# A hybrid decoder layer on one core: the decays' mask moves to GpSimd, the memory's transposes are issued later, and the last stage multiplies before its norm

## The chip, the cores and the metric

One Trainium2 chip, of which one core is used. The metric is the device time of one execution in microseconds (us). It is the median of three runs, and one further execution was profiled.

## The reference, cut to what matters

One decoder layer on x (1 x 1024 x 1024, float32): a root-mean-square norm, a projection to eleven parts, three branches (gated DeltaNet, differential attention, cross-attention to a memory of 256 rows), a gated sum, an output projection and a norm with the residual added.

```python
h = rms_norm(x, pre_w)
(gdn_qkv, gdn_a, gdn_b, gdn_z, dq, dk, dv, dz, mq, mz, gate_logits) = [h @ w_in[:, lo:hi] for lo, hi in bounds]
qkv = jax.nn.silu(causal_depthwise_conv(gdn_qkv, conv_w))
...
# inside the gated DeltaNet, by chunks
G = jnp.cumsum(gc, axis=-1)
gamma = jnp.exp(jnp.where(incl, G[..., :, None] - G[..., None, :], -jnp.inf))
a_low = jnp.where(strict, bc[..., :, None] * kk * gamma, 0.0)
...
attn_intra = jnp.einsum("bnhcd,bnhed->bnhce", qc, kc) * gamma
...
m = rms_norm(mem, mem_norm_w)
mk, mv = jnp.split(m @ w_mem_kv, 2, axis=-1)
...
out = y @ w_out
return x + rms_norm(out, post_w)
```

`gamma` is the masked decay that the first part of the change is about, `m` the memory's norm of the second, and the last line the third.

## The kernel before, in words

The sequence of 1024 positions lies along the free axis of most tiles, features along the 128 partitions. The program goes through stages on one core: the input projections with the DeltaNet of 8 heads (to about 550 us), the memory's norm, keys and values (about 550 to 590 us), the attention projections, the attention and the branches' merge, and the output projection with its norm (from about 1840 us).

**Projections.** `gemm` (L209) multiplies a weight block of 128 columns with the normed input into one of two PSUM tiles `acc` (128 x 1024). A weight block is loaded in two pieces (`wr`), and `wsplit` (L161) splits each piece in two for precision: ACT casts the high part `wh` (L167), DVE subtracts for the low part `wl` (L169). The products of `wh` are L219 and L220, those of `wl` L224; one weight column block of 128 rows takes four 512-column matmuls of `wh` and then two of `wl`. So PE can start a gemm with `wh` alone and needs `wl` after four matmuls.

**Heads.** `conv_head` (L430) evacuates such an `acc`: ACT writes the first tap (L435), DVE adds three more taps reading the same PSUM tile (L437, three instructions one after the other), ACT applies SiLU (L439). `key`, `qry` and `val` do that for the key, query and value of each head. Beside a key or query runs a thread (`key_side`, `qry_side`): `decay` (L461) loads the cumulative decays of a head into a 128 x 1024 tile by DMA (L463), waits two steps, adds the mask `mneg` on DVE (L465), waits a step, and ACT takes eight exponentials (L468, one per chunk of 128). `chunk_products` (L470) lets PE multiply chunks into a PSUM tile `sd` (L474), DVE multiplies by the decays (L476) and sums diagonals (L480). There are 8 heads with 2 decays each, so 16 masks. `squares` transposes on PE (L449) and squares on ACT (L457). POOL (GpSimd) computes powers (`rpow`, L158) and products with a whole tile: L504 (a key's decays times `fj`), L629 (a query times a decay), L691 and L692 (power and product at the end of a pair of heads' scan). `inverses` (L512) solves on DVE with many small instructions (L528, L529).

**What sets the order.** The threads are generators. `count` (L183) advances all of them one step whenever six big matmuls have been issued, and `pause(n)` (L201) lets n steps pass. Then a scheduler orders each engine's instructions, so that they don't stand in the order of the code: an engine runs its own list in order, and a later instruction waits behind an earlier one that isn't ready. A change of engine or pause therefore moves neighbours too.

**Memory.** `mem_norm` (L744) loads two tiles of 128 rows (`raw`), ACT squares, POOL raises to a power (L158), DVE scales (L760); after `pause(3)` (L762) PE transposes the tiles in 16 instructions (L767), ACT and DVE split the result (L771, L772). `mem_keys` and `mem_values` use it (L784, L795 to L797). The threads of `combine_tokens` (L818 to L828 on POOL and DVE, then L742 on DVE) work beside it.

**Last stage.** For each of 8 tiles of 128 rows PE fills two halves `po` (128 x 512, PSUM); ACT squares each half with a sum (L1438), DVE adds the sums (L1440), POOL raises to -1/2 (L1441), and for each half DVE multiplies with the norm and the weight (L1443); the residual is added by POOL for half 0 and DVE for half 1 (L1444), and a DMA writes the half (L1445).

Of the kernel before, what the change touches and what calls it, by code (L numbers as in the profile page):

```python
# [9 lines left out]
F32 = mybir.dt.float32  # L10
F32R = mybir.dt.float32r
AF = mybir.ActivationFunctionType
ALU = mybir.AluOpType
# [3 lines left out]
P = 128  # L17
# [7 lines left out]
NEG = -1.0e30  # L25
# [20 lines left out]
def bm(ap, m):  # L46

    return ap.unsqueeze(1).to_broadcast([ap.shape[0], m, ap.shape[1]])
# [3 lines left out]
def hybrid_layer_kernel(  # L52
# [10 lines left out]
    def pool(name, bufs=1, space=None):  # L63
        kw = {} if space is None else {"space": space}
        return tc.tile_pool(name=name, bufs=bufs, **kw)
# [4 lines left out]
    op = ctx.enter_context(pool("op"))  # L70
# [40 lines left out]
    def sd():  # L111
        return sidp.tile([P, 4, P], F32, name=nm("sd"), tag="sd", bufs=4)

    def small(shape, tag, bufs=2, dt=F32):
        return sm.tile(list(shape), dt, name=nm(tag), tag=tag, bufs=bufs)
# [4 lines left out]
    V, A, G, T = nc.vector, nc.scalar, nc.gpsimd, nc.tensor  # L120
# [80 lines left out]
    def pause(n):  # L201
        for _ in range(n):
            yield
# [72 lines left out]
    with gx:  # L276
        gp = gx.enter_context(pool("gp"))
# [7 lines left out]
        tri = gp.tile([P, P], F32, name="tri")  # L285
        G.memset(tri, 1.0)
        G.affine_select(tri, tri, pattern=[[1, P]], compare_op=ALU.is_ge, fill=0.0, base=0, channel_multiplier=-1)
        mneg = gp.tile([P, P], F32, name="mneg")
        G.memset(mneg, 0.0)
        G.affine_select(mneg, mneg, pattern=[[1, P]], compare_op=ALU.is_ge, fill=NEG, base=0, channel_multiplier=-1)  # L290
        ones = gp.tile([P, P], F32, name="ones")
        G.memset(ones, 1.0)

# [167 lines left out]
        def decay(h, gm):  # L461

            nc.sync.dma_start(gm, gscr[0, 8 * h:8 * h + 8, :].rearrange("c i -> (c i)").partition_broadcast(P))  # L463
            yield from pause(2)
            V.tensor_tensor(gm, gm, bm(mneg, 8), op=ALU.add)  # L465
            yield from pause(1)
            for c in range(8):
                A.activation(gm[:, c], gm[:, c], AF.Exp, bias=negG[:, h, c:c + 1])  # L468
# [253 lines left out]
    def xtile(shape=(P, S), dt=F32):  # L722
        return xp.tile(list(shape), dt, name=nm("x"), tag="x", bufs=9)

    def rtile(shape=(P, S), dt=F32):
        return xp.tile(list(shape), dt, name=nm("raw"), tag="raw", bufs=3)
# [8 lines left out]
    SUB, ADD, MUL = ALU.subtract, ALU.add, ALU.mult  # L735
# [8 lines left out]
    def mem_norm():  # L744

        mts = []
        for t in range(2):
            mt = rtile((P, D))
            nc.sync.dma_start(mt, mem[t * P:(t + 1) * P, :])
            mts.append(mt)  # L750
        for _ in range(2):
            mh.append(xtile((P, 4, MEM), F32R))
            ml.append(xtile((P, 4, MEM), F32R))
        sq = rtile()
        for mt in mts:
            ss = small([P, 1], "ss", 4)
            A.activation(sq, mt, AF.Square, accum_out=ss)
            rs = small([P, 1], "rs", 4)
            rpow(rs, ss, 1.0 / D, EPS, mhalf)
            V.tensor_scalar(mt, mt, rs, None, op0=MUL)  # L760
            yield
        yield from pause(3)  # L762
        for k2 in range(4):
            pt = sd()
            for kk in range(2):
                for t in range(2):
                    T.transpose(pt[:, 2 * kk + t], mts[t][:, (2 * k2 + kk) * P:(2 * k2 + kk + 1) * P], ident)  # L767
            for kk in range(2):
                k = 2 * k2 + kk
                src = pt[:, 2 * kk:2 * kk + 2].rearrange("p a b -> p (a b)")  # L770
                A.activation(mh[k // 4][:, k % 4], src, AF.Copy, scale=memw[:, k:k + 1])  # L771
                V.scalar_tensor_tensor(ml[k // 4][:, k % 4], src, memw[:, k:k + 1],  # L772
                                       mh[k // 4][:, k % 4].bitcast(F32), op0=MUL, op1=SUB)
            yield
        ready.add("mem")
# [294 lines left out]
    base = xtile()  # L1070
# [341 lines left out]
    pw = xtile()  # L1412
# [16 lines left out]
    for t in range(NT):  # L1429

        ts_ = slice(t * P, (t + 1) * P)
        po = pos[t] if t < 2 else columns()
        xr, res = xtile(), xtile()
        nc.sync.dma_start(xr, x[ts_, :])
        ss = small([P, 2], "oss", 4)
        for f, sl in enumerate(half):
            products(po, t, range(4 if t < 2 else 0, KT), f)
            A.activation(res[:, sl], po[f], AF.Square, scale=1.0 / 32, accum_out=ss[:, f:f + 1])  # L1438
        rs = small([P, 1], "rs", 4)
        V.tensor_scalar(rs, ss[:, 0:1], ss[:, 1:2], EPS, op0=ADD, op1=ADD)  # L1440
        G.tensor_tensor(rs, rs, mhalf[:, 0:1], op=ALU.pow)  # L1441
        for f, sl in enumerate(half):
            V.scalar_tensor_tensor(res[:, sl], po[f], rs, pw[:, sl], op0=MUL, op1=MUL)  # L1443
            (V if f else G).tensor_tensor(res[:, sl], res[:, sl], xr[:, sl], op=ADD)  # L1444
            nc.sync.dma_start(out[ts_, sl], res[:, sl])  # L1445


# [22 lines left out]
```

## Time and profile before

| | |
|---|---|
| median of three runs | 1926.06 us (1922.33 to 1928.35) |
| the profiled execution | 1924.15 us |
| its span in the trace | 1922.4 us |
| mean granted TensorE clock | 0.992 of full speed |
| busy PE (matmul) | 1868.7 us, 97% of the span |
| busy DVE | 1218.5 us, 63% |
| busy ACT | 894.5 us, 47% |
| busy POOL | 164.0 us, 9% |

The span is from the first to the last instruction of the profiled execution; its own time is 1.75 us longer. PE is TensorE's matmul, DVE VectorE, ACT ScalarE, POOL GpSimd, SP the engine whose queue issues the DMAs. Busy time overlaps between engines. A wait is an engine's idle time, put down to the work that ended it.

### The profile page before, as it was taken

The numbers are of one execution on the slowest core, as the hardware profiler recorded it, in microseconds if no ns is written. First come the engines' busy times: TensorE is split into PE (matmuls) and PEld (weight loads), VectorE is DVE, ScalarE is ACT, GpSimd is POOL, SyncE is SP. The second block draws the span as 40 slices with busy tenths as digits, with TensorE's granted clock in tenths as the row PEclk, the third lists the DMA queues.
The fourth block names the chain that finished last, engine by engine and source line by source line (L and its number), as shares of the span: only waits on it lengthen the run. The fifth ranks groups of instructions, "written<-read, shape, count | busy, mean of one in ns | idle before, by whom it ended". The sixth has DMA issues, their size and how long they took to land.

```text
span 1922.4 us, 28495 instructions
## 1 busy us (share of the span) xinstructions
PE 1868.7 (97%) x10231; PEld 1561.9 (81%) x10231; DVE 1218.5 (63%) x2499; ACT 894.5 (47%) x1997; POOL 164.0 (9%) x131
## 2 busy tenths in 40 slices
PE   7999999999978999999999999999999999999998
PEld 5787888788866888888888888888888878888886
DVE  5688667855366676777777777766666662435432
ACT  5552664545444465555555565555444551212211
POOL 1130131302140100000000000000000000000011
PEclk9999999999989999999999999999999999999999
DMA  4232231322136675656657355443665586755422
GB/s 129 87 97 68 69 96 42 98 63 75 51 120 200 190 210 171 173 162 184 185 143 212 114 176 170 148 154 104 214 207 188 170 270 206 231 195 171 156 91 88
DMA packets 294018, 282.45 MB, mean 147 GB/s; under 512 B 41474, under 2 KB 226164, under 8 KB 293876
## 3 DMA queue, kind: packets, MB, share of 16 engines
q1 hardware_dynamic: 293876, 280.63, 47.4%
q8 instruction: 80, 1.31, 0.3%
q14 instruction: 62, 0.51, 0.1%
HBM read 189.27 MB, written 91.29 MB: 146 GB/s over the span
## 4 chain that ended last, share of the span: by engine, by line
PE 57%; issue 30%; DVE 8%; ACT 2%; DMA 2%; POOL 1%; SPq 0%; POOLq 0%; DVEq 0%; ACTq 0%
PE bank L878 27%; PE acc L224 4%; PE acc L220 4%; PE acc L219 4%; PE sd L1191 3%; PE sd L1143 2%; PE sd L1142 2%; PE sd L1176 2%; DVE o L437 1%; DVE wl L169 1%; PE sd L474 1%; DMA wr<-in_w_mem_kv_dram 1%; PE sd L661 1%; PE sd L673 1%; PE sd L668 1%
## 5 line engine op out<-in xcount | busy, mean ns | idle before, releaser
L878 PE MATMUL bank<-h,hi 128*128 128x512 f32 x864 | 283.7, 398 | 0.0
L167 ACT CAST wh<-wr 128x512 fp32r<-128x512 f32 x144 | 89.3, 620 | 281.6 <-PE acc L220 251.6
L219 PE MATMUL acc<-h,wh 128*128 128x512 f32 x468 | 194.1, 415 | 2.2 <-DVE rp L157 1.8
L220 PE MATMUL acc<-h,wh 128*128 128x512 f32 x468 | 186.7, 399 | 0.0
L878 PE MATMUL bank<-q,hi 128*128 128x512 f32 x576 | 186.4, 397 | 0.0
L878 PE MATMUL bank<-o,hi 128*128 128x512 f32 x576 | 185.2, 396 | 0.8 <-DVE u L965 0.4
L878 PEld LDWEIGHTS bank<-h,hi 128*128 128x128 f32 x864 | 159.5, 188 | 28.2
L878 PE MATMUL bank<-h,lo 128*128 128x512 f32 x432 | 171.4, 397 | 0.0
L224 PE MATMUL acc<-h,wl 128*128 128x512 f32 x468 | 159.4, 399 | 9.2 <-DVE wl L169 9.2
L169 DVE TENSOR_TENSOR wl<-wr,wh 128x512 fp32r<-128x512 f32 x144 | 102.7, 714 | 101.3 <-ACT wh L167 97.8
L864 ACT CAST hi<-wr 128x512 fp32r<-128x512 f32 x144 | 89.0, 618 | 133.2 <-PE bank L878 112.9
L868 DVE TENSOR_TENSOR lo<-wr,hi 128x512 fp32r<-128x512 f32 x144 | 98.9, 687 | 52.8 <-PE bank L878 39.8
L878 PEld LDWEIGHTS bank<-o,hi 128*128 128x128 f32 x576 | 106.4, 188 | 22.1 <-ACT u L883 1.2
L878 PEld LDWEIGHTS bank<-q,hi 128*128 128x128 f32 x576 | 107.0, 188 | 19.9
L878 PE MATMUL bank<-q,lo 128*128 128x512 f32 x288 | 114.5, 398 | 0.0
L878 PE MATMUL bank<-o,lo 128*128 128x512 f32 x288 | 114.2, 396 | 0.0
L224 PEld LDWEIGHTS acc<-h,wl 128*128 128x128 f32 x468 | 88.4, 191 | 29.1 <-DVE wl L169 11.3
L1158 ACT ACTIVATE x<-x,ng 128x256 f32<-128x256 f32 (+7 forms) x128 | 98.8, 774 | 24.7 <-DVE ng L1154 24.7
L864 ACT CAST hi<-raw 128x512 fp32r<-128x512 f32 x108 | 66.9, 619 | 84.9 <-PE bank L878 79.6
L219 PEld LDWEIGHTS acc<-h,wh 128*128 128x128 f32 x468 | 89.3, 191 | 17.4 <-issue 3.0
L220 PEld LDWEIGHTS acc<-h,wh 128*128 128x128 f32 x468 | 89.3, 191 | 14.5
L878 PEld LDWEIGHTS bank<-h,lo 128*128 128x128 f32 x432 | 81.4, 188 | 14.2
(361 smaller groups left out, 4125.3 us busy)
## 6 DMA issues: line engine op xcount, KB each, us to landing
raw<-in_w_in_dram SPq DMA_DIRECT2D x144, 256.0 KB, 3.8
wr<-in_w_in_dram SPq DMA_DIRECT2D x64, 256.0 KB, 2.8
qd<-u SPq DMA_DIRECT2D x128, 128.0 KB, 2.4
wl<-qd SPq DMA_DIRECT2D x64, 256.0 KB, 3.5
gts<-u SPq DMA_DIRECT2D x48, 256.0 KB, 3.2
u<-oscr SPq DMA_DIRECT2D x48, 256.0 KB, 4.6
raw<-gts SPq DMA_DIRECT2D x24, 512.0 KB, 4.4
o<-gscr SPq DMA_DIRECT2D x16, 512.0 KB, 4.9
```

What stands on the lines that cost most here:

```text
L167: A.copy(hi, raw)
L169: V.tensor_tensor(lo, raw, hi.bitcast(F32), op=ALU.subtract)
L219: T.matmul(ps[:, sl], lhsT=hi[:, kk], rhs=hh(k, f), start=(k == 0), stop=False)
L220: T.matmul(ps[:, sl], lhsT=hi[:, kk], rhs=hl(k, f), start=False, stop=False)
L224: T.matmul(ps[:, sl], lhsT=lo[:, kk], rhs=hh(k, f), start=False, stop=(k == 7))
L864: A.copy(self.hi[p], self.src[p])
L868: V.tensor_tensor(self.lo[p], self.src[p], self.hi[p].bitcast(F32), op=SUB)
L878: T.matmul(ps, lhsT=t[l][:, kk], rhs=comb[p][kk][r], start=(first and kk + n == 0), stop=(kk == 3 and n == 2), skip_group_check=True)
L1142: T.matmul(ps[m], lhsT=q4[:, m], rhs=ks[m][:, u:e], start=True, stop=False)
L1143: T.matmul(ps[m], lhsT=q4[:, 2 + m], rhs=ks[m][:, u:e], start=False, stop=True)
L1158: A.activation(s[i][m][:, :w], s[i][m][:, :w], AF.Exp, bias=ng[:, m:m + 1], scale=scl, accum_out=l)
L1191: T.matmul(po[:, 0], lhsT=pT[:, c], rhs=vt[:, c], start=(c == 0), stop=(c == i))
```

## The change

Three edits. (1) The mask of the decays: `affine_select` on POOL, which fills the masked places with the large negative constant, takes the place of the addition of `mneg` on DVE; the tile `mneg` and its two setup instructions go. (2) `mem_norm` waits nine steps instead of three ahead of its transposes. (3) In the last stage DVE multiplies each half with the weight as soon as the half is there, ACT then squares the half in place in PSUM, and after the norm one DVE instruction per half multiplies by it and adds the residual; POOL's and DVE's additions go.

```diff
--- before.py
+++ after.py
@@ -285,9 +285,6 @@
         tri = gp.tile([P, P], F32, name="tri")
         G.memset(tri, 1.0)
         G.affine_select(tri, tri, pattern=[[1, P]], compare_op=ALU.is_ge, fill=0.0, base=0, channel_multiplier=-1)
-        mneg = gp.tile([P, P], F32, name="mneg")
-        G.memset(mneg, 0.0)
-        G.affine_select(mneg, mneg, pattern=[[1, P]], compare_op=ALU.is_ge, fill=NEG, base=0, channel_multiplier=-1)
         ones = gp.tile([P, P], F32, name="ones")
         G.memset(ones, 1.0)
 
@@ -462,7 +459,8 @@
 
             nc.sync.dma_start(gm, gscr[0, 8 * h:8 * h + 8, :].rearrange("c i -> (c i)").partition_broadcast(P))
             yield from pause(2)
-            V.tensor_tensor(gm, gm, bm(mneg, 8), op=ALU.add)
+            G.affine_select(gm, gm, pattern=[[0, 8], [1, P]], compare_op=ALU.is_ge, fill=NEG, base=0,
+                            channel_multiplier=-1)
             yield from pause(1)
             for c in range(8):
                 A.activation(gm[:, c], gm[:, c], AF.Exp, bias=negG[:, h, c:c + 1])
@@ -759,7 +757,7 @@
             rpow(rs, ss, 1.0 / D, EPS, mhalf)
             V.tensor_scalar(mt, mt, rs, None, op0=MUL)
             yield
-        yield from pause(3)
+        yield from pause(9)
         for k2 in range(4):
             pt = sd()
             for kk in range(2):
@@ -1435,13 +1433,13 @@
         ss = small([P, 2], "oss", 4)
         for f, sl in enumerate(half):
             products(po, t, range(4 if t < 2 else 0, KT), f)
-            A.activation(res[:, sl], po[f], AF.Square, scale=1.0 / 32, accum_out=ss[:, f:f + 1])
+            V.tensor_tensor(res[:, sl], po[f], pw[:, sl], op=MUL)
+            A.activation(po[f], po[f], AF.Square, scale=1.0 / 32, accum_out=ss[:, f:f + 1])
         rs = small([P, 1], "rs", 4)
         V.tensor_scalar(rs, ss[:, 0:1], ss[:, 1:2], EPS, op0=ADD, op1=ADD)
         G.tensor_tensor(rs, rs, mhalf[:, 0:1], op=ALU.pow)
         for f, sl in enumerate(half):
-            V.scalar_tensor_tensor(res[:, sl], po[f], rs, pw[:, sl], op0=MUL, op1=MUL)
-            (V if f else G).tensor_tensor(res[:, sl], res[:, sl], xr[:, sl], op=ADD)
+            V.scalar_tensor_tensor(res[:, sl], res[:, sl], rs, xr[:, sl], op0=MUL, op1=ADD)
             nc.sync.dma_start(out[ts_, sl], res[:, sl])
```

Lines of the changed kernel are two to three lower than those of the kernel before (L435 is L432, L437 is L434, L439 is L436, L457 is L454, L468 is L466, L480 is L478, L691 is L689, L767 is L765); the select is L462. A tile's number in the listings counts allocations.

The order on ACT between the query and the value of head 0, about 99 to 116 us of the trace before. In these rows `o` is first the query's tile (L435, L439) and then two decay tiles (the query's own and a key's), `e` a tile of squares, `v` the value's tile and `wh` the high part of a weight piece. Before:

```order
L435 ACTIVATE o_957<-acc_853,cols 128x1024
L167 CAST wh_1114<-wr_1112 128x512
L439 ACTIVATE o_957<-o_957 128x1024
L468 ACT_TABLE_LOAD
L468 ACTIVATE o_980<-o_980,negG 128x128 x8
L457 ACTIVATE e_1017<-sd_1012 128x512
L457 ACTIVATE e_1038<-sd_1033 128x512
L468 ACTIVATE o_994<-o_994,negG 128x128 x8
L167 CAST wh_1162<-wr_1160 128x512
L435 ACTIVATE v_1105<-acc_963,cols 128x1024
L167 CAST wh_1219<-wr_1217 128x512
```

With the change:

```order
L432 ACTIVATE o_958<-acc_852,cols 128x1024
L466 ACT_TABLE_LOAD
L466 ACTIVATE o_981<-o_981,negG 128x128
L436 ACT_TABLE_LOAD
L436 ACTIVATE o_958<-o_958 128x1024
L466 ACT_TABLE_LOAD
L466 ACTIVATE o_981<-o_981,negG 128x128 x7
L454 ACTIVATE e_1020<-sd_1015 128x512
L454 ACTIVATE e_1043<-sd_1038 128x512
L466 ACTIVATE o_995<-o_995,negG 128x128 x8
L432 ACTIVATE v_1110<-acc_964,cols 128x1024
L167 CAST wh_1119<-wr_1117 128x512
```

The cast of the gemm that comes next on PE (`wh_1114`, now `wh_1119`) stood behind the query's first tap and ahead of the decays; now it stands behind both decays' exponentials and behind the value's first tap. Two more table loads stand there.

The order on DVE at the same place with the change, from the value's taps on:

```order
L434 SCALAR_TENSOR_TENSOR v_1110<-acc_964,cols,v_1110 128x1023
L478 ISA sd_1081,ssk_1060<-sd_1081,ident 128x128
L478 ISA ssk_1060 128x1
L434 SCALAR_TENSOR_TENSOR v_1110<-acc_964,cols,v_1110 128x1022
L499 TENSOR_SCALAR fj<-ssk_1060 128x8
L157 TENSOR_SCALAR rp_1101<-ssk_1060 128x8
L434 SCALAR_TENSOR_TENSOR v_1110<-acc_964,cols,v_1110 128x1021
L500 RECIPROCAL fj<-fj 128x8
L169 TENSOR_TENSOR wl_1121<-wr_1117,wh_1119 128x512
```

The subtraction for that same gemm (`wl_1121`, whose high part is `wh_1119`) stands behind the three taps of the value. Before the change it stood ahead of them, right behind the two mask additions L465.

The order on POOL at the end of the first scan, about 262 to 272 us of the trace before, with the change:

```order
L690 TENSOR_TENSOR v_1110<-v_1110,sso_1871 128x1024
L689 TENSOR_TENSOR sso_1872<-sso_1872,mhalf 128x8
L690 TENSOR_TENSOR v_1338<-v_1338,sso_1872 128x1024
L462 AFFINE_SELECT o_2525<-o_2525 128x1024
L462 AFFINE_SELECT o_2648<-o_2648 128x1024
```

The select of a later key's decays (`o_2525`) is queued behind the powers and products of the scan's end; before the change that mask was an addition on DVE.

The order on PE at the memory's transposes. Before:

```order
L767 MATMUL sd_5317<-ident,raw_5250 128x128
L767 MATMUL sd_5332<-ident,raw_5250 128x128
L219 MATMUL acc_5237<-h_137,wh_5293 128x512
L220 MATMUL acc_5237<-h_138,wh_5293 128x512
L219 MATMUL acc_5237<-h_137,wh_5293 128x512
L220 MATMUL acc_5237<-h_138,wh_5293 128x512
L767 MATMUL sd_5317<-ident,raw_5252 128x128
L767 MATMUL sd_5317<-ident,raw_5250 128x128
```

With the change:

```order
L220 MATMUL acc_5363<-u_130,wh_5366 128x512
L224 MATMUL acc_5363<-h_128,wl_5368 128x512
L224 MATMUL acc_5363<-u_129,wl_5368 128x512
L765 MATMUL sd_5402<-ident,raw_5277 128x128
L765 MATMUL sd_5402<-ident,raw_5279 128x128
L765 MATMUL sd_5402<-ident,raw_5277 128x128
L765 MATMUL sd_5402<-ident,raw_5279 128x128
L219 MATMUL acc_5363<-h_131,wh_5416 128x512
```

Ahead of the first transpose now stand 30 more 512-column matmuls, the last block of the gemm in hand (`acc_5237`, now `acc_5264`) and the first half of the next (`acc_5363`); and the transposes of the two memory tiles now alternate from the first on.

## Rows read from the trace of the kernel before

**Rows 1.** PE's waits, whole span: who waited, for what, us in total, times, longest.
```profile
PE acc L224 <- DVE wl L169: 9.2, 4, 4.5
...
PE sd L767 <- issue: 9.0, 1, 9.0
...
PE acc L796 <- DVE wl L169: 4.5, 4, 2.9
...
PE acc L219 <- DVE rp L157: 1.8, 1, 1.8
```

**Rows 2.** DVE and PE by time, 69 to 78 us: start, length, instruction, [idle before].
```profile
69.83 1.28 DVE L437 SCALAR_TENSOR_TENSOR y<-acc,cols,y 128x1023 f32<-128x1023 f32 x1
...
74.70 0.79 PE L224 MATMUL acc<-h,wl 128*128 128x512 f32 x1 [3.49 <-DVE wl L169]
...
77.00 0.63 PE L220 MATMUL acc<-u,wh 128*128 128x512 f32 x1
```

**Rows 3.** ACT and POOL by time, 101 to 113 us.
```profile
104.02 0.62 ACT L167 CAST wh<-wr 128x512 fp32r<-128x512 f32 x1 [3.80 <-PE acc L220]
...
105.63 1.28 ACT L468 ACT_TABLE_LOAD   x1
...
106.92 2.46 ACT L468 ACTIVATE o<-o,negG 128x128 f32<-128x128 f32 x8
...
109.28 1.05 ACT L457 ACTIVATE e<-sd 128x512 f32<-128x512 f32 x2
...
110.24 2.44 ACT L468 ACTIVATE o<-o,negG 128x128 f32<-128x128 f32 x8
...
101.77 1.64 POOL L158 TENSOR_TENSOR nk<-rp,phalf 128x8 f32<-128x8 f32 x1 [19.20 <-DVE rp L157]
```

**Rows 4.** DVE by time, 111 to 120 us.
```profile
111.54 0.69 DVE L476 TENSOR_TENSOR o<-sd,o 128x512 f32<-128x512 f32 x1 [0.16 <-ACT o L468]
...
115.23 1.28 DVE L437 SCALAR_TENSOR_TENSOR v<-acc,cols,v 128x1023 f32<-128x1023 f32 x1
...
119.16 0.19 DVE L502 RECIPROCAL fj<-fj 128x8 f32<-128x8 f32 x1
```

**Rows 5.** PE by time, 114 to 116 us.
```profile
114.32 0.39 PE L224 MATMUL acc<-h,wl 128*128 128x512 f32 x1
...
114.78 1.05 PE L474 MATMUL sd<-o,y 128*128 128x128 f32 x8
```

**Rows 6.** Lines L465 and L1075: ns of one (least, median, most), first and last start.
```profile
L465 DVE TENSOR_TENSOR o<-o,mneg x16: 1204/1224/2918, 62.6 to 442.3; 128x1024 f32<-128x1024 f32 x16
...
L1075 POOL TENSOR_SCALAR_AFFINE_SELECT x<-x x1: 1149/1149/1149, 634.8 to 634.8; 128x1024 f32<-128x1024 f32 x1
```

**Rows 7.** POOL and DVE by time, 142 to 147 us.
```profile
142.32 1.29 POOL L629 TENSOR_TENSOR o<-o,e 128x512 f32<-128x512 f32 x1 [1.88 <-DMA e<-gscr]
...
142.68 1.18 DVE L529 TENSOR_TENSOR q<-q,y 128x220 f32<-128x220 f32 x1
...
146.48 0.38 DVE L529 TENSOR_TENSOR q<-q,y 128x231 f32<-128x231 f32 x1
```

**Rows 8.** POOL and ACT by time, 266 to 271 us.
```profile
268.72 1.90 POOL L692 TENSOR_TENSOR v<-v,sso 128x1024 f32<-128x1024 f32 x1
...
267.18 2.45 ACT L468 ACTIVATE o<-o,negG 128x128 f32<-128x128 f32 x8 [3.12 <-DVE o L465]
```

**Rows 9.** DVE by time, 556 to 560 us.
```profile
556.61 0.75 DVE L760 TENSOR_SCALAR raw<-raw,rs 128x1024 f32<-128x1024 f32 x1 [1.67 <-POOL rs L158]
...
558.48 0.75 DVE L760 TENSOR_SCALAR raw<-raw,rs 128x1024 f32<-128x1024 f32 x1 [0.45 <-POOL rs L158]
```

**Rows 10.** Busy us by window: length, PE, PEld, DVE, ACT, POOL; granted clock, DMA share, GB/s.
```profile
550.00:600.00 50.00, 36.51 (x142) 27.24 (x142) 43.56 (x58) 22.99 (x43) 18.79 (x13) 0.86 0.46 141
```

**Rows 11.** All engines by time at the kernel's end.
```profile
1915.01 0.60 ACT L1438 ACTIVATE x<-sd 128x512 f32<-128x512 f32 x1 [4.63 <-PE sd L1419]
...
1918.05 1.20 DVE L1444 TENSOR_TENSOR x<-x,x 128x512 f32<-128x512 f32 x1
```

## The prediction

> **What bounds the kernel.** I read the profile table first: PE is busy 97% of the span, so work taken from DVE, ACT or POOL pays only where PE waits for it. The waits of PE say where that is [rows 1]. About 25 us stand in four groups: gemms that wait for the low part of their weights (`wl`, 9.2 and 4.5 us), one wait of 9.0 us ahead of the memory's transposes, and one of 1.8 us for an `acc` tile. The masks are named nowhere in it. The reader should see that ACT and DVE reach PE by their order: both run their lists in order, and a cast for the next gemm that stands behind the evacuation of the last one comes late. The trace has one clear case. At 69.83 DVE begins the three taps of a key (L437); the subtraction for the gemm already begun stands behind them, and PE idles 3.49 us until 74.70 [rows 2]. The order of before has that pattern once in this stage, with 2.2 us of PE work between the two gemms' neighbouring rows. The order of the change has it three times, the old one and two new.
>
> **Part 1, the mask.** It takes 16 additions from DVE, 1.224 us each by the median, 19.6 us in all, and gives POOL 16 selects [rows 6]. The trace has one select of that shape, 1.149 us, on another tile; I take that. Setup loses two small instructions that nothing waits for: nothing. As PE names no wait for a mask, I count none of the 19.6 us as a direct gain. What counts is the order that follows.
>
> *First place, about 115 us.* Before, the cast `wh` of the next gemm ran at 104.02, ahead of the decays [rows 3]. It now comes after both groups of exponentials and the value's first tap. POOL's power ends at 103.4, so the query's select ends near 104.6; then ACT does one exponential (0.3), a table load (1.28), SiLU (1.0, what lies between the cast and the load before) and another load, and the other seven (2.15) end at 110.6 where the eight ended at 109.4. With the squares (1.05) the key's exponentials start near 111.6, not 110.24: 1.4 us later. DVE's product L476 waits for them; it began at 111.54, so the value's taps start at 116.6 instead of 115.23, and after the 3.93 us that the three took, the reciprocal behind them (0.2) and 0.7 for the subtraction (as long as L476, of the same shape) the new `wl` is there at 121.4 [rows 4]. PE needed it at 114.32; with a group of short products now ahead (0.8 of the 1.05) it comes there at about 115.1 [rows 5]. So 6.3 us of new idle time. The wait costs more than its length: after the 3.49 us a matmul at 77.00 still took 0.63 us, where one takes 0.39 at 114.32 [rows 2, 5], as if at the lower of the clock's two levels, 1.2 in place of 2.4 GHz. Two such matmuls start 0.46 apart at the full clock [rows 5]; some 6 at half lose 6 x 0.2 = 1.2 us. Here I put 1.5. **+7.8 us.**
>
> *Second place, about 25 us later.* The same pattern with the query of head 1. From the query's first tap ACT and DVE need 1.1 (tap, about as SiLU), 4.0 (three taps), 1.3 (solve steps between them), 1.28, 1.0, 1.28, 2.15, 1.05, 1.1 and 0.6 to the next `wh`: 14.9 us. PE has 48 matmuls at 0.23 and about 24 to 32 short ones at 0.1, 13.4 us, and meets another us of waiting for `wl`. An estimate from [rows 3 to 5]: **+2.5 us**, between 0 and 5.
>
> *Third place, about 272 us.* The exponentials of a key started at 267.18, behind a mask on DVE. Its select now stands on POOL behind the products of the scan's end, the last of which ends at 270.62; with 1.15 it is out at 271.8, 4.6 us later [rows 8]. ACT evacuates the last gemm's `acc` right behind those exponentials, and PE's wait of 1.8 us for that tile [rows 1] grows by as much. **+4.6 us.** There are places like it near 350 us and later; in them I see slack and put nothing, leaving them to the upper end.
>
> Sum of part 1: 7.8 + 2.5 + 4.6 = **+14.9 us**. From below: had ACT and DVE slack in all of it, -2. From above, with the late places and the full 18.4 us of selects felt by DVE, +24.
>
> *A rule against it.* While POOL's L629 ran from 142.32 to 143.61, a DVE subtraction of 128x220 with two SBUF inputs took 1.18 us from 142.68, to just behind POOL's end; one of 128x231 with POOL idle took 0.38 [rows 7]. The Trainium skill (SBUF — State Buffer, "SBUF: two separate sides") says that DVE with two SBUF inputs and a GpSimd instruction that reads SBUF share a port pair that one of them holds for its whole instruction, so that the other blocks fully. By that rule, the trace agrees: 0.8 us were lost. In the sum by the row alone a select costs DVE at most its 1.15 us; 16 of them give back 18.4 of the 19.6 us.
>
> **Part 2, the transposes.** PE stood 8.97 us and resumed at 557.57. The transposes wait for the scaled memory tiles, and DVE scales them when POOL's power is out: the first starts at 556.61, the second at 558.48, 0.75 us each [rows 9]. PE does not enter into that, so these moments stay. The 30 matmuls now ahead take 30 x 0.23 = 6.9 us; the transposes alternate, so PE waits for the second tile too, to 559.2, and idles some 3.5 us in place of 9. Gain 5.5, and about 1.5 from the clock, granted at 0.86 in this window [rows 10]. But DVE is busy 43.56 of the 50 us here [rows 10], and the memory's products wait for `wl` again behind it (4.5 us [rows 1]). They come 6 us sooner while DVE's list is no shorter. I take back 3. **-4 us**, between 0 and -9.
>
> **Part 3, the last stage.** Only the last of 8 tiles lies on the path. There a DVE product of about 0.7 now stands between PE's end and the square at 1915.01, and the addition of 1.20 at 1918.05 goes, with the wait behind POOL's own [rows 11]. **-0.7 us**, between -1.5 and 0; in the other seven PE's next tile covers it, and if that cover went each would cost the 0.7.
>
> **Sum.** 14.9 - 4 - 0.7 = +10.2 us on the profiled execution's 1924.15: **1934 us**. That execution lies 1.9 us below the median of the runs shown, inside their spread.
>
> **Rivals.**
>
> *The casts are in time.* If the orders leave more slack than I read (a `wh` may run while PE is still on the gemm before), part 1 is worth -2 to +1 and the rest stays: 1924.15 - 4 to -7 - 0.7 = about 1918 us with half of the memory's gain given back. For it: DVE loses 19.6 us in a stage where it is the engine PE waits for. Against: the pattern at 74.70 [rows 2]. It decides at the first place: if `wl` is there at 115 us, this is the case. This is the rival on the other side.
>
> *One new wait, one lost.* The first place alone is real (+8), the third is hidden, the memory gives 7 and the end 0.7: 1924 to 1929 us, no change. For it: the third place lies where PE has other work of the scan.
>
> *The selects hold DVE.* Each of the 16 delays a DVE cast or tap by up to 1.15 us, as in [rows 7]; if a third of them lie ahead of a late cast, that adds 6 us to my sum: 1940 us. Against: in many places POOL starts when the DMA lands, with DVE on PSUM inputs. The skill's rule on the shared port pair, named above, is this rival's.
>
> *The later transposes do nothing.* If DVE's list bounds the memory stage altogether, part 2 is 0: 1938 us, within the forecast's range.
>
> **Chances.** My forecast 0.35, the selects 0.10, no gain from the memory 0.08: slower, 0.53. One wait for one, no change: 0.22. Casts in time, faster: 0.25. A measurement of this kernel can tell about 0.3%, 5.8 us, from no change. The range takes in the rival on the fast side and part 1's upper bound with some of the memory's gain: 1916 to 1945. The slower cases alone would give 1931 to 1945.
>
> **What would show it.** Right: a PE wait for `wl` of 4 us or more near 115 to 122 us, with one for `wh` ahead of it; a wait for `acc` near 275 that grew to about 6; the wait ahead of the transposes at 2 to 4 us in place of 9, with more waiting in the memory's products behind it. Wrong: no PE wait above 2 us between 100 and 150, or the exponentials of the first scan's end still starting near 267 us. If the waits of PE in the first 550 us add to no more than before, part 1 was mis-read and the first rival has it.

## The result and the profile after

The changed kernel took 1937.87 us as the median of five runs (1935.13 to 1942.02), the kernel before 1927.85 beside it (1922.33 to 1928.35). The ratio is **1.0061 [1.0046, 1.0075]**: slower by 0.6%, about 12 us between the means of the runs (10.0 between the medians). The forecast was 1934 in 1916 to 1945. The profiled execution shown below took 1937.87 us, with a span of 1936.2 us and a granted clock of 0.988.

The first part of the profile's page of the changed kernel: busy us of each engine, share of the span, instructions.

```profile
PE 1874.2 (97%) x10231; PEld 1567.5 (81%) x10231; DVE 1200.9 (62%) x2491; ACT 902.1 (47%) x2003; POOL 166.1 (9%) x137
```

DVE has 17.6 us less to do than before, POOL 2.1 more, and the kernel is longer. What grew is PE's waiting. The waits of PE in the changed kernel (who waited for what, us in total, times, longest):

```profile
PE acc L224 <- DVE wl L169: 12.5, 5, 4.4
...
PE acc L793 <- ACT wh L167: 6.0, 2, 4.3
PE acc L794 <- DVE wl L169: 4.5, 4, 3.4
...
PE acc L219 <- ACT wh L167: 3.8, 3, 1.8
PE acc L219 <- DVE rp L157: 3.3, 1, 3.3
...
PE sd L765 <- DVE raw L758: 1.5, 1, 1.5
```

Against [rows 1]: the waits for a gemm's `wl` rose from 9.2 to 12.5 (3.2 of these lie in the memory stage, further down), waits for `wh` are new (3.8), and the 9.0 ahead of the transposes is 1.5. But the memory's keys now wait 6.0 for `wh` at L793, where they waited 2.1 before (L795 there). In the first 545 us all of PE's waits make 31.6 us, and made 23.3 before. So the trace has a loss in that stretch, and a gain in the memory stage that came back as another wait.

**The first place.** ACT by time in the changed kernel, 106 to 119 us:

```profile
106.87 0.40 ACT L466 ACTIVATE o<-o,negG 128x128 f32<-128x128 f32 x1 [2.97 <-POOL o L462]
107.29 1.28 ACT L436 ACT_TABLE_LOAD   x1
...
113.98 2.44 ACT L466 ACTIVATE o<-o,negG 128x128 f32<-128x128 f32 x8
116.32 1.10 ACT L432 ACTIVATE v<-acc,cols 128x1024 f32<-128x1024 f32 x1
117.32 1.13 ACT L167 CAST wh<-wr 128x512 fp32r<-128x512 f32 x2
```

DVE by time, 118 to 124 us:

```profile
121.55 1.27 DVE L434 SCALAR_TENSOR_TENSOR v<-acc,cols,v 128x1021 f32<-128x1021 f32 x1
...
122.85 0.64 DVE L169 TENSOR_TENSOR wl<-wr,wh 128x512 fp32r<-128x512 f32 x1
```

PE by time, 117 to 125 us:

```profile
117.98 0.50 PE L219 MATMUL acc<-h,wh 128*128 128x512 f32 x1 [1.24 <-ACT wh L167]
...
118.78 0.39 PE L220 MATMUL acc<-u,wh 128*128 128x512 f32 x1
123.54 0.79 PE L224 MATMUL acc<-h,wl 128*128 128x512 f32 x1 [4.37 <-DVE wl L169]
124.13 0.63 PE L224 MATMUL acc<-u,wl 128*128 128x512 f32 x1
```

The reader should follow one weight piece. Its cast `wh` ran at 104.02 before [rows 3]. Now it runs at 117.32, behind the exponentials of two decays and the value's first tap on ACT, and PE waits 1.24 us for it. Its subtraction stands behind the value's three taps on DVE and runs at 122.85, and PE waits 4.37 more. Afterwards a matmul takes 0.63 us where it took 0.39, the mark of the clock's lower level: the granted clock is 0.52 from 123.54 to 129.54.

Where a gemm's first tap on ACT (L435, now L432) follows the gemm at once, it tells how late the program is. Three such taps, one ahead of the place, one behind it and one behind the next place. Before, and then in the changed kernel:

```profile
99.11 1.11 ACT L435 ACTIVATE o<-acc,cols 128x1024 f32<-128x1024 f32 x1
...
127.10 1.11 ACT L435 ACTIVATE o<-acc,cols 128x1024 f32<-128x1024 f32 x1
...
165.24 1.11 ACT L435 ACTIVATE y<-acc,cols 128x1024 f32<-128x1024 f32 x1
```

```profile
101.48 1.11 ACT L432 ACTIVATE o<-acc,cols 128x1024 f32<-128x1024 f32 x1
...
137.57 1.11 ACT L432 ACTIVATE o<-acc,cols 128x1024 f32<-128x1024 f32 x1
...
177.85 1.11 ACT L432 ACTIVATE y<-acc,cols 128x1024 f32<-128x1024 f32 x1
```

The program is 2.4 us late ahead of the place and 10.5 us behind it. (The value's own taps, at 116.32 and 150.48, can't be used: there ACT comes late itself, behind the exponentials and squares.) This place costs **8.1 us**: 5.6 of waiting, and some 2.5 of matmuls that start 0.43 us apart instead of 0.23.

**The second place.** PE by time, 151 to 155 us: the same pattern with smaller waits, 2.1 us together. At 177.85 the program is 12.6 us late, where it was 10.5: **2.1 us**.

```profile
152.14 0.50 PE L219 MATMUL acc<-h,wh 128*128 128x512 f32 x1 [0.77 <-ACT wh L167]
...
154.68 0.50 PE L224 MATMUL acc<-h,wl 128*128 128x512 f32 x1 [1.34 <-DVE wl L169]
```

**The third place.** POOL and ACT by time, 275 to 281 us:

```profile
275.37 1.90 POOL L690 TENSOR_TENSOR v<-v,sso 128x1024 f32<-128x1024 f32 x1
277.23 3.19 POOL L462 TENSOR_SCALAR_AFFINE_SELECT o<-o 128x1024 f32<-128x1024 f32 x3
...
278.35 2.45 ACT L466 ACTIVATE o<-o,negG 128x128 f32<-128x128 f32 x8 [6.67 <-POOL o L462]
```

The selects do stand behind the scan's last product on POOL. But the program is 11.7 us late here, so on the clock of before the exponentials begin at 278.35 - 11.7 = 266.65, against 267.18 [rows 8]. PE waits more at the spot (3.3 us for `rp`, which was 1.8 [rows 1], and 1.75 for a `wh` at 282, which is new), yet the gemms' first taps are 11.72 us late at 237.23 and 11.68 at 295.85. Between these two taps PE has 306 matmuls to do, where it had 339, so part of the scan's work was done earlier and makes room for the waits. From one tap to the other this place costs nothing.

**The memory stage.** PE by time in the changed kernel, 564 to 593 us:

```profile
564.65 0.50 PE L224 MATMUL acc<-h,wl 128*128 128x512 f32 x1 [1.82 <-DVE wl L169]
...
571.34 0.55 PE L765 MATMUL sd<-ident,raw 128*128 128x128 f32 x3 [1.52 <-DVE raw L758]
...
574.22 1.22 PE L224 MATMUL acc<-h,wl 128*128 128x512 f32 x2 [1.41 <-DVE wl L169]
...
588.80 0.80 PE L793 MATMUL acc<-wh,x 128*128 128x512 f32 x1 [4.34 <-ACT wh L167]
592.97 0.80 PE L794 MATMUL acc<-wl,x 128*128 128x512 f32 x1 [3.38 <-DVE wl L169]
```

The wait of 9.0 us became four (1.82, 1.52, 1.41 and 4.34: 9.1 us), and the last one, 3.38, was 2.9 before [rows 1]. The stage's rows in the view of PE's waits, added (from 545 us to 655, the later end since the program is late), make 17.1 us before and 17.1 after. The window of [rows 10], in the changed kernel (length, PE, PEld, DVE, ACT, POOL; granted clock, DMA share, GB/s):

```profile
550.00:600.00 50.00, 37.51 (x150) 28.94 (x149) 43.24 (x53) 22.98 (x42) 25.49 (x18) 0.83 0.41 121
```

The clock is no better (0.83, 0.86 before). At the first product of the next stage (L878, now L876) the program is 13.0 us late, so the memory stage gave nothing and cost about 1.

**The kernel's end.** All engines by time: DVE's product, then ACT's square in PSUM.

```profile
1929.12 0.69 DVE L1436 TENSOR_TENSOR x<-sd,x 128x512 f32<-128x512 f32 x1 [4.75 <-PE sd L1417]
1929.91 0.58 ACT L1437 ACTIVATE sd<-sd 128x512 f32<-128x512 f32 x1 [4.75 <-DVE x L1436]
```

From here to the span's end are 1936.2 - 1929.12 = 7.1 us. Before, from the square at 1915.01 [rows 11] to 1922.4, it was 7.4: 0.3 us gained.

### The profile page after: what moved, and what is told of

Its sections match the earlier page's. It is cut to its first block, busy times and chain, and to the rows that moved or that the text cites. A ratio compares the mean times of both kernels' runs of the same rounds, so it can differ in the third digit from the quotient of the medians.

```text
span 1936.2 us, 28510 instructions
## 1 busy us (share of the span) xinstructions
PE 1874.2 (97%) x10231; PEld 1567.5 (81%) x10231; DVE 1200.9 (62%) x2491; ACT 902.1 (47%) x2003; POOL 166.1 (9%) x137
## 4 chain that ended last, share of the span: by engine, by line
PE 82%; DVE 8%; issue 3%; ACT 3%; DMA 2%; POOL 1%; SPq 0%; DVEq 0%; POOLq 0%; ACTq 0%
PE bank L876 31%; PE acc L219 9%; PE acc L224 9%; PE acc L220 8%; PE sd L1417 4%; PE sd L1189 3%; PE sd L1141 2%; PE sd L1140 2%; PE sd L1174 2%; PE sd L1291 1%; PE sd L1258 1%; PE sd L472 1%; DVE wl L169 1%; PE sd L659 1%; PE sd L671 1%
## 5 line engine op out<-in xcount | busy, mean ns | idle before, releaser
L876 PE MATMUL bank<-h,hi 128*128 128x512 f32 x864 | 283.7, 398 | 0.0
L876 PE MATMUL bank<-q,hi 128*128 128x512 f32 x576 | 186.5, 397 | 0.0
L876 PE MATMUL bank<-o,hi 128*128 128x512 f32 x576 | 185.2, 396 | 1.0 <-DVE u L963 0.7
L876 PEld LDWEIGHTS bank<-h,hi 128*128 128x128 f32 x864 | 159.5, 188 | 28.2
L224 PE MATMUL acc<-h,wl 128*128 128x512 f32 x468 | 160.1, 401 | 12.5 <-DVE wl L169 12.5
L876 PE MATMUL bank<-h,lo 128*128 128x512 f32 x432 | 171.5, 397 | 0.0
L876 PEld LDWEIGHTS bank<-o,hi 128*128 128x128 f32 x576 | 106.4, 188 | 22.3 <-ACT u L881 1.2
L876 PEld LDWEIGHTS bank<-q,hi 128*128 128x128 f32 x576 | 107.0, 188 | 19.9
L876 PE MATMUL bank<-q,lo 128*128 128x512 f32 x288 | 114.5, 398 | 0.0
L876 PE MATMUL bank<-o,lo 128*128 128x512 f32 x288 | 114.1, 396 | 0.0
L876 PEld LDWEIGHTS bank<-h,lo 128*128 128x128 f32 x432 | 81.4, 188 | 14.1
```

The lines of the kernel that those rows point to most:

```text
L224: T.matmul(ps[:, sl], lhsT=lo[:, kk], rhs=hh(k, f), start=False, stop=(k == 7))
L876: T.matmul(ps, lhsT=t[l][:, kk], rhs=comb[p][kk][r], start=(first and kk + n == 0), stop=(kk == 3 and n == 2), skip_group_check=True)
```

## The experiments

The theory: the loss is all part 1's, and comes from the order it brings (casts behind evacuations), not from the select's length; part 2's wait only moved. The rivals: the selects hold DVE; the parts act on each other; the memory stage waits because DVE's list is too long.

### The three parts alone

Part 1 alone is the first hunk of the change and the lost tile (e1), and e2 has all but this:

```diff
-            V.tensor_tensor(gm, gm, bm(mneg, 8), op=ALU.add)
+            G.affine_select(gm, gm, pattern=[[0, 8], [1, P]], compare_op=ALU.is_ge, fill=NEG, base=0,
+                            channel_multiplier=-1)
```

Part 3 alone (e3) is the last stage's hunk, and part 2 alone (e7) the pause:

```diff
-            A.activation(res[:, sl], po[f], AF.Square, scale=1.0 / 32, accum_out=ss[:, f:f + 1])
+            V.tensor_tensor(res[:, sl], po[f], pw[:, sl], op=MUL)
+            A.activation(po[f], po[f], AF.Square, scale=1.0 / 32, accum_out=ss[:, f:f + 1])
...
-            V.scalar_tensor_tensor(res[:, sl], po[f], rs, pw[:, sl], op0=MUL, op1=MUL)
-            (V if f else G).tensor_tensor(res[:, sl], res[:, sl], xr[:, sl], op=ADD)
+            V.scalar_tensor_tensor(res[:, sl], res[:, sl], rs, xr[:, sl], op0=MUL, op1=ADD)
```

```diff
-        yield from pause(3)
+        yield from pause(9)
```

Part 1 alone:

> The kernel before with part 1 alone: the masks are selects on POOL; pause and last stage as before. The order of the first 545 us is that of the changed kernel. Order theory: the whole loss is here, the cumulated delay of the changed kernel at 500 us, some 11 us (10.8 after taking off the 0.9 us by which its first gemms already began later): 1936 to 1940 us, with PE waits of 1.2 + 4.4 us near 118 and 124 us. Rival (the loss is shared by parts 2 or 3): under 1932 us.

Parts 2 and 3 without part 1:

> The kernel before with parts 2 and 3 and without part 1; the order of the first 545 us is that of before. My prediction's term: 4.7 us less than before, about 1922. What the trace of the changed kernel says (its waits from 550 to 620 us add up to as much as before): the 9.0 us wait goes and comes back as waits for wh and wl in the memory's products, 1925 to 1928 us, no change.

Part 3 alone:

> The kernel before with part 3 alone; everything ahead of the last stage is in the order of before. The prediction's term is -0.7 us, the trace of the changed kernel says -0.3 from PE's last end to the end of the span: same as before within 2 us. Rival: the wait of the square for DVE delays PE's next tile through the PSUM tiles, up to 0.7 us in each of 8 tiles: +5 us.

Part 2 alone:

> The kernel before with part 2 alone. The scheduler makes another order of the DeltaNet stage of it too: the cast behind three taps near 75 us is gone, and two weaker cases of a wh and a wl behind the evacuation of the gemm before stand near 250 and 310 us, with 2 to 4 us of PE work in between. Order theory: no wait at 75 us, waits of 1 to 3 us near 250 and 310; the memory stage as in the kernel without the mask's edit, 2 us slower than before: 1921 to 1930 in all. Rival (such patterns in the order say nothing of PE's waits): the wait of 3.5 us near 75 us stays.

| kernel | median us | before, beside it | ratio |
|---|---|---|---|
| part 1 alone | 1937.38 | 1925.74 | 1.0063 [1.005, 1.0075] |
| parts 2 and 3 | 1929.03 | 1925.74 | 1.0016 [1.0006, 1.0026] |
| part 3 alone | 1925.35 | 1925.74 | 1.0004 [0.9994, 1.0013] |
| part 2 alone | 1930.9 | 1927.39 | 1.0012 [1.0003, 1.002] |

Part 1 alone loses what the whole change loses, some 12 us. Its PE waits near 117, 123, 152 and 154 us have the lengths of the changed kernel's (1.22, 4.36, 0.74 and 1.36 us), and its wait ahead of the transposes is the old 8.97. Part 3 can't be told from nothing. Part 2, whose 9 us were the largest wait in the middle of the kernel, costs 2 to 3 us; both kernels that have it without part 1 say so, and both lie about 1 us above the ranges expected. Part 1 alone and the other two alone add up to some 15 us where the whole took 12; the intervals are too wide to tell that from a plain sum, so a small action of the parts on each other is not excluded. What the expectation of part 2 alone says of the order in the first 545 us is wrong: its order there is that of before, and the wait near 75 us stays (4.44 us), so nothing that it says on that is borne out.

PE's waits in the kernel with parts 2 and 3 show where the 9 us went:

```profile
PE acc L795 <- ACT wh L167: 6.0, 2, 4.4
PE acc L796 <- DVE wl L169: 5.2, 5, 3.4
...
PE sd L767 <- DVE raw L760: 1.5, 1, 1.5
```

Over the stage they add to 17.2 us, where the kernel before has 17.1.

### Is it the order, or the select?

Part 1 with one step more between the mask and the exponentials (e4), so that the order changes and the selects stay; and the kernel before with the same step more, the masks still on DVE (e8).

e4, against part 1 alone:

```diff
                             channel_multiplier=-1)
-            yield from pause(1)
+            yield from pause(2)
             for c in range(8):
```

e8, against the kernel before:

```diff
             V.tensor_tensor(gm, gm, bm(mneg, 8), op=ALU.add)
-            yield from pause(1)
+            yield from pause(2)
             for c in range(8):
```

> Part 1 alone, with two steps instead of one between the select and its exponentials. The 16 selects are the same; the scheduler's order is another one, in which no new weight cast stands behind the evacuation of the gemm before it (only the old case near 75 us is left). Order theory: the 11 us go, PE waits near 118 and 124 us are gone, 1922 to 1930 us. Rival (POOL's selects hold DVE, or ACT waits for them wherever they stand): the loss stays, 1935 us or more.

> The kernel before, masks on DVE, with two steps instead of one between mask and exponentials. Order theory: the time follows the order, whoever makes the mask. Here the case near 75 us (3.5 us and its slow matmuls, some 5 us) is gone and the two weaker cases are there: 1919 to 1926 us, faster than before if those are hidden. Rival (the order's changes cancel, only the engine of the mask counts): same as before.

e4 took 1933.41 us, 1.0037 [1.0024, 1.0051]; e8 1934.94 us, 1.0037 [1.0025, 1.005]. As in the experiment before, what e8's expectation says of the order and of the wait near 75 us is wrong: that wait stays, at 3.85 us. PE's waits of e4:

```profile
PE sd L446 <- ACT o L436: 6.6, 2, 4.0
...
PE acc L224 <- DVE wl L169: 5.8, 3, 3.6
```

With the selects kept and the order changed, the waits of part 1 near 118, 124 and 152 us are gone: the longest left for a gemm's `wl` is the old one near 75 us (3.6), and the first tap at 319.23 is 0.7 us ahead of before. So those waits come from the order, as the theory says. But e4 is 3.3 us late at 438.62, where PE waits 4.02 and 2.02 us at 360 and 370 (before 4.46 once), and 6.4 late at the first product after the memory. The first of these losses can be chance: part 3 alone, whose order there is that of before, is 3.8 us late at the same tap of its profiled execution. e4 landed between the two theories' numbers. e8, with the masks on DVE, missed both of its own, and lands at the ratio of e4: with the longer pause it makes no difference which engine has the mask. With the pause of before it does (part 1 alone, 12 us), through the order. Where a step more loses its 7 us was not tried further.

### What holds the memory stage

First the rival that DVE's list is too long. The 16 subtractions of `combine_tokens` were taken off DVE (zeros by POOL in place of the low parts), with part 3 and with the pause at 3 (e5) and at 9 (e6).

```diff
-                split(t[:, 0], t[:, 1], src)
+                A.copy(t[:, 0], src)
+                G.memset(t[:, 1].bitcast(F32), 0.0)
```

> The kernel before with the last stage's edit, and with the DVE subtractions in combine_tokens (L742, 16 low parts) left out: POOL fills those low parts with zeros, so that part of the computation is changed. pause(3) as before. Theory (DVE's list bounds the memory stage): some 16 x 0.7 to 1.8 us of DVE work go from 545 to 600 us; the wait ahead of the transposes stays at 5 us or more, since it is the norm's own chain, and the waits for wl in the memory's products (2.9 + 1.0 us) go: 3 to 8 us below before. Rival (DVE's list does not matter here): same as before.

> The same with pause(9). Theory (the later transposes gain only where DVE has room): the wait ahead of the transposes falls to under 3 us and no wait of 3 us or more takes its place in the products, so it is 4 to 7 us faster than the same kernel with pause(3). Rival (the transposes' move gives nothing even then): within 2 us of it.

e5 took 1924.44 us, 0.9987 [0.9978, 0.9996]; e6 1930.08, 1.0008 [0.9999, 1.0017]. In e5 the products' long waits for `wl` went, as the rival has it (L796 0.4 us in all), but the wait ahead of the transposes grew to 11.35; and in e6 the later transposes lose 0.2% where they should have gained. The waits of the stage add to 15.1 and 15.7 us. This speaks against the rival, but POOL got the fills in exchange, so it is e11 below, with more work on DVE, that settles it. DVE and POOL of e6 by time, 561 to 569 us, show something else:

```profile
561.22 2.23 DVE L760 TENSOR_SCALAR raw<-raw,rs 128x1024 f32<-128x1024 f32 x1 [0.47 <-POOL rs L158]
...
565.88 2.21 DVE L760 TENSOR_SCALAR raw<-raw,rs 128x1024 f32<-128x1024 f32 x1 [0.68 <-POOL rs L158]
```

```profile
561.16 1.28 POOL L819 TENSOR_TENSOR hi<-h 128x512 f32<-128x512 f32 x1
562.38 0.52 POOL L833 MEMSET o<- 128x512 f32 x1
```

The scaling of a memory tile, 0.75 us in [rows 9] with POOL idle, takes 2.2 beside POOL's addition and fill. So POOL's work, and not only DVE's own list, makes DVE late. Two kernels then held `combine_tokens` back until the memory's transposes were done, from its third (e9) or its second (e10) of four rounds on, with parts 2 and 3. The four one-column copies only make the dependency. Shown is e9; e10 has 1 in place of both 2s.

```diff
+            if j == 2:
+                while "mem" not in ready:
+                    yield
+            if j >= 2:
+                for b in (b12, b11, b22, b21):
+                    V.tensor_copy(b[:, 0:1], ml[1][:, 3, MEM - 1:MEM].bitcast(F32))
```

> Parts 2 and 3 without part 1, as in the run without the mask, and the second half of combine_tokens made to wait, by a small copy that depends on it, for the memory's split. Theory (what the 9 us wait turned into is the order on ACT and DVE: the split of the transposes, L771 and L772, stood behind casts of combine_tokens that wait for POOL and DVE): the waits of 4.4 and 3.4 us for wh and wl in the memory's products go, 5 to 9 us below the same kernel without the gate: 1920 to 1924. Rival (the transposes come too late in any order): within 2 us of it, 1927 to 1931.

> The same with three quarters of combine_tokens behind the memory's split, so that the norm's power and scale are not behind its additions either. Theory: as the run with one half gated, and the wait ahead of the transposes is under 1.5 us: 1916 to 1922, unless the work put off comes back as waits of the first attention projections near 615 to 640 us, which would show there. Rival: 1927 us or more.

e9 took 1925.76 us, 0.9986 [0.9977, 0.9995], some 0.3% below the kernel with parts 2 and 3 alone; e10 1928.17, 0.9998 [0.9989, 1.0007]. Both missed their theory's range. In e9 waits of 3.0 and 4.1 us take the place of the 4.4 and 3.4, and the stage's waits add to 15.2. In e10 the wait at the transposes is gone altogether, and the waits of the stage still add to 17.4 us. DVE of e10 by time shows the next cause:

```profile
584.76 1.73 DVE L830 TENSOR_TENSOR hi<-hi,hi 128x512 f32<-128x512 f32 x1 [2.35 <-POOL hi L825]
586.41 1.75 DVE L169 TENSOR_TENSOR wl<-wr,wh 128x512 fp32r<-128x512 f32 x1
```

DVE stands 2.35 us for a sum that POOL hasn't finished, with a weight's subtraction queued behind it, and both then run beside POOL at 1.7 us each where such an instruction takes 0.68. That points at a cause under the shifting waits: the additions of `combine_tokens` on POOL. The last two kernels move them to DVE, with part 3, at a pause of 3 (e11) and of 9 (e12).

```diff
-            G.tensor_tensor(b12, f32(u0[:, :]), f32(u1[:, :]), op=ADD)
-            G.tensor_tensor(b11, f32(b1[:, 0]), f32(b1[:, 1]), op=ADD)
+            V.tensor_tensor(b12, f32(u0[:, :]), f32(u1[:, :]), op=ADD)
+            V.tensor_tensor(b11, f32(b1[:, 0]), f32(b1[:, 1]), op=ADD)
             for b, sl in ((b22, slice(512, 1024)), (b21, slice(0, 512))):
-                G.tensor_tensor(b, f32(b2h[:, sl]), f32(b2l[:, sl]), op=ADD)
+                V.tensor_tensor(b, f32(b2h[:, sl]), f32(b2l[:, sl]), op=ADD)
```

> The kernel before with the last stage's edit, and combine_tokens' 16 additions (L818 to L821) on DVE, not POOL; pause(3). Handoff theory (in the memory stage DVE's list stands still at combine_tokens' subtractions, which wait for POOL's additions, and its instructions with two SBUF inputs are held while POOL adds, 1.75 in place of 0.68 us): DVE gets 16 x 0.7 = 11 us more work but loses the waits and the stretching; the wait ahead of the transposes is under 6 us and those for wl in the products under 2 us in all: 1918 to 1924. Length theory (only the amount of DVE work counts): 5 us or more slower than before, 1930 or more.

> The same with pause(9). Handoff theory: with POOL out of the way the later transposes give what I had counted, 2 to 6 us less than the same kernel with pause(3): 1914 to 1920. Theory that the transposes' move only shifts a wait: within 2 us of it. Length theory: 1930 or more.

e11 took **1913.61 us, 0.9933 [0.992, 0.9946]**, and e12 1912.72, 0.993 [0.9916, 0.9945]: both beat the kernel before and the changed one, e11 by more than the 1918 to 1924 expected. The window of [rows 10] in e11, and then DVE's groups by line from 545 to 615 us (instructions, busy us, mean ns of one, idle before):

```profile
550.00:600.00 50.00, 45.19 (x201) 33.59 (x200) 47.00 (x80) 28.82 (x52) 1.87 (x2) 1.00 0.60 180
```

```profile
L821 DVE TENSOR_TENSOR hi<-h,h 128x512 f32<-128x512 f32 x8 | 5.2, 681 | 0.0
L742 DVE TENSOR_TENSOR q<-hi,q 128x512 fp32r<-128x512 f32 x6 | 4.0, 683 | 0.0
L742 DVE TENSOR_TENSOR o<-hi,o 128x512 fp32r<-128x512 f32 x6 | 4.0, 682 | 0.0
```

The same groups in the kernel before:

```profile
L742 DVE TENSOR_TENSOR o<-hi,o 128x512 fp32r<-128x512 f32 x6 | 9.5, 1580 | 0.0
L742 DVE TENSOR_TENSOR q<-hi,q 128x512 fp32r<-128x512 f32 x6 | 6.2, 1042 | 0.0
```

DVE does 16 additions more at 0.68 us each, and its 12 subtractions of L742 alone give back 15.7 - 8.0 = 7.7 us. PE runs 201 matmuls in the window instead of 142, at full clock. The waits of the stage add to 7.5 us (e12: 7.0), not 17.1: of the 13.6 us gained, 9.6 are waits, and the rest fits the clock, 1.00 where it was 0.86. The place is right too: e11 is 3.9 us behind the trace before at the last first tap (439.19) and 10.9 ahead at the first product after the memory (603.56). So the length of DVE's list is out as the cause, and POOL's additions are what makes the waits; how much is the waiting for POOL's results and how much the stretched instructions, these runs don't separate. The two kernels lie within 1 us of each other: with the additions moved, PE waits 1.1 us in all at the transposes of e11, and there is little left for a later start to save.

## Why the prediction held, and where it did not

The forecast of slower held, and 1934 us is 0.2% below the median measured. It said 10.2 us more than the profiled execution before; measured are 10 (medians) to 12 (means). Its first reason was right, and two of its terms were wrong with opposite signs.

*Part 1, first place: right.* The prediction said 7.8 us (6.3 idle, 1.5 clock); it is 8.1 (5.6 idle, some 2.5 clock). The program came to this place 2.4 us late already. With 2.4 us taken off, the key's exponentials start at 113.98 - 2.4 = 111.6 (said 111.6), and `wl` is there at 123.49 - 2.4 = 121.1 (said 121.4). The wait is split, 1.24 for `wh` and 4.37 for `wl`, since the late `wh` holds PE first. The rival that the casts are in time is out.

*Part 1, second place: right.* 2.5 said, 2.1 measured.

*Part 1, third place: wrong.* The step "another 4.6 us later" took the scan's end on POOL to stay where it was against the gemms. It came sooner: the first power of the pair starts at 270.08, 7.6 us later than the 262.45 of before where the gemms are 11.7 later. Its second power took 1.64 us, where it was 2.62. So against the scan the exponentials are 3.6 us late, near the 4.6 said, and against the gemms they are not. That the scan gained because DVE has no masks is argued, not shown.

*Part 1, later places: not seen.* The prediction found the pattern once in the order of before. But the longest wait for `wl` in [rows 1], 4.5 us, is another, at 365.41, with the subtraction on DVE behind products, a sum and a query's first tap. With part 1 it is gone, and PE waits 4.1 us at 369.82 for a query's SiLU (L436), which stands on ACT behind an exponential that waited 7.0 us for a select. The two make up for each other (the first taps are 11.6 us late at 356.05 and 11.4 at 400.42), so the nothing that the prediction put there came out by luck.

*The selects hold DVE: no.* The 16 selects take 1.09 to 1.55 us, 1.096 in the middle (said 1.149):

```profile
L462 POOL TENSOR_SCALAR_AFFINE_SELECT o<-o x16: 1093/1096/1549, 64.2 to 449.6; 128x1024 f32<-128x1024 f32 x16
```

Beside the two selects from 105.74 on, DVE ran the query's last tap, which reads PSUM, at the usual 1.28. And e4 with the selects takes as long as e8 without them.

*Part 2: wrong.* The gain of 5.5 + 1.5 less 3 was -4; part 2 alone measured +2 to +3. The wait ahead of the transposes shrank as said (1.5 us left, 2 to 4 said), but the step "I take back 3" was far too small: all of it came back. The prediction saw that DVE's list would be no shorter. It did not see that POOL's additions made DVE late, whatever PE did first. In the changed kernel DVE's L822 ran 1.75 us beside POOL, ACT stood 6.79 us for its result with the splits of the transposes and the next `wh` queued behind, and PE waited 4.34 us for that. ACT by time, 580 to 589 us:

```profile
580.51 0.62 ACT L739 CAST q<-hi 128x512 fp32r<-128x512 f32 x1 [6.79 <-DVE hi L822]
581.04 0.47 ACT L769 ACTIVATE x<-sd,cols 128x256 fp32r<-128x256 f32 x1
...
588.13 0.61 ACT L167 CAST wh<-wr 128x512 fp32r<-128x512 f32 x1
```

The rival "the later transposes do nothing" was the right one for this part, with the wrong engine named.

*Part 3: right in size.* -0.7 said, -0.3 in the trace, not to be told from nothing in the runs.

*The sum.* Part 1 measured about 12 us where 14.9 was said, part 2 +2 to +3 where -4 was said: the errors of 3 and 6 us partly cancel, so that the number came out better than the reasoning behind it, and that much is luck. The two places that part 1 shows make 10.2 us; of the 13.7 us between the two profiled executions 2.4 were there ahead of both: 0.9 from the first 45 us, ahead of any select, and 1.5 of clock after the old wait near 75 us (below), which is no part of the change.

Open: where the kernels with a step more lose their 7 us; and what part 1 is worth with the additions moved, which was not tried.

## What to carry to other kernels

A change that frees a busy engine can still lose when the bottleneck waits for the order and not for the work: follow one late operand back through the in-order lists of two engines, and count what now stands ahead of it. A wait that ends at a transfer between two other engines need not go when the waiting step is moved; add up the waits of the whole stage, and if the sum stays, look for the pair of engines that hand work to each other or slow each other. Here additions on the lightly loaded POOL cost more than they saved, and moving them to the busier DVE gave 0.7%.

## What the runs showed of the hardware

*DVE beside POOL.* Two-input DVE subtractions of 128 x 512 in SBUF took 0.68 us with POOL quiet and 1.58 in the mean beside POOL's additions; the reverse holds too: POOL's product L504 took 2.72 us while DVE added masks (two of them 4.05 us, 2 x 1.224 when alone), and the same product 1.90 us when they were gone. And a DVE instruction with only one SBUF tile as input (L760) took 2.2 in place of 0.75. The Trainium skill (SBUF — State Buffer, "SBUF: two separate sides") describes one port pair that DVE and GpSimd hold in turn: for a DVE instruction with two SBUF inputs against a GpSimd instruction that reads SBUF, and for one in a 2-port performance mode. With the first the trace agrees, 0.68 to 1.58 us, as in [rows 7]; the 0.75 to 2.23 us of L760 fit the second, but the trace doesn't show in which mode that instruction ran. The Trainium skill (GPSIMD Engine Reference, "4.1 Engine selection") puts an addition of two tiles on VectorE, as GpSimd is about twice as slow; the trace agrees, 1.5 to 1.6 us on POOL in the mean of the kernel before and 0.68 on DVE.

*The clock after a wait.* The same wait near 75 us is followed by a slow stretch of different length from one execution to the next. The 14 us from the wait's end, in the kernel before and then in the one with parts 2 and 3, whose order is the same there (columns as above):

```profile
74.70:88.70 14.00, 14.00 (x56) 11.48 (x57) 8.40 (x28) 6.14 (x7) 6.83 (x4) 0.90 0.35 79
```

```profile
74.93:88.93 14.00, 14.00 (x49) 11.29 (x50) 5.85 (x27) 5.70 (x7) 6.82 (x4) 0.78 0.34 76
```

In the 14 kernels profiled here the granted clock of this stretch lies between 0.78 and 0.90, and the kernel before was profiled at the upper end. Seven matmuls fewer in 14 us, at 0.23 us each, are 1.6 us, and a term of that size in a comparison of two profiled executions can be chance.
